# Moving the first stage's arithmetic off GpSimd in a hybrid DeltaNet/HGRN2 step: convolution by pairs of blocks, norm_w folded into x

## The chip, the cores and the metric

One core of a Trainium2 chip runs the whole program. Its engines are the tensor engine (PE, with its weight loads as PEld), the vector engine (DVE), the scalar engine (ACT), GpSimd (POOL) and the sync engine (SP), which here issues every DMA that the program names. Each engine runs its own list of instructions in a fixed order and waits on semaphores. The metric is device time of one execution in microseconds (us).

## The reference, cut to what matters

One layer on a prompt of 4096 tokens (32 tiles of 128) and on a sample of 8 sequences of 16 tokens (one more tile), all in float32. The input x is normed, projected, and split over two groups of heads, whose outputs are joined by one output projection.

```python
h = _rmsnorm(x, norm_w)                   # x * rsqrt(mean(x^2) + eps) * norm_w
proj = h @ w_in
qkv, z_a, b_a, a_a, hq, hf, hi, z_b = jnp.split(proj, offs, axis=-1)
qkv_c = silu(causal depthwise conv of width 4 of qkv)          # 1536 channels
q_a, k_a = l2norm(q) * 64 ** -0.5, l2norm(k)                   # 8 heads of 64
beta, g = sigmoid(b_a), -exp(A_log) * softplus(a_a + dt_bias)
# group A, chunk by chunk, per head: G = cumsum(g), decay[i, j] = exp(G_i - G_j) for i >= j
lower = strict(beta * (k k^T) * decay)
u, w = solve(I + lower, [beta * v, beta * k * exp(G)])
v_new = u - w S;   o = (q * exp(G)) S + ((q k^T) * decay) v_new
S = S * exp(G_last) + (k * exp(G_last - G))^T v_new
# group B (HGRN2): gated linear attention of 4 heads of 128, its own state
y = x + concat(rmsnorm(o_a) * silu(z_a), rmsnorm(o_b) * silu(z_b)) @ w_out;  out = rmsnorm(y)
```

## The kernel before, in words

The program has two phases. **Phase A** norms x, projects q, k, v and the gates of group A, convolves, and runs the delta rule; it also prepares the weights of the second phase. **Phase B** runs HGRN2, the gates and the output projection. Weights and activations are cut into high and low float16 parts, so that a product is three float16 matmuls (`mm3`).

Phase A works on groups: one for the sample tile, then 16 groups of two prompt tiles. For a group g its loop (L285 to L323) issues, in this order of the code: the load and norm of x for g+2 (`xload`), the recurrence of g-1 (`gdn_rec`), decays and score matrices of g (`gdn_pre`), the triangular inverses of g (`gdn_inv`), the transposes of x for g+2 (`xtrans`), the second half of the preparation (`gdn_pre2`), the gates of g+2, the projection and convolution of g+1 (`proj`), and six steps of `wspill`, which reads weights of phase B, scales them and writes their float16 parts to DRAM. A scheduler then puts the instructions of each engine into the order in which the engine runs them; so pieces of neighbouring groups are interleaved, and a small edit can move much.

Names that recur:

- `proj`, L484 to L515: for each of 12 blocks of 128 channels, 24 matmuls into `acc` (L462 to L464). ACT copies the scaled `acc` into `u` (L493) behind three columns of the tile before (`halo`, POOL), makes the tap on the current token from `acc` (`c`, L504) and the oldest tap (`c0`, L507); POOL adds the two (L508); DVE adds the two middle taps (L510); ACT makes the tanh (L512) and DVE the SiLU (L514). `u`, `c`, `c0` and `acc` have two buffers each.
- `gdn_pre`, L517: `E`, [128, 8 heads, 128], comes by a broadcast DMA with G along its free axis; POOL subtracts G of the partition's token (L539) and masks with -1000 (L540); ACT exponentiates (L547). ACT sums squares of k head by head (L554, 8 instructions, each with a read of its accumulator). DVE multiplies the scores by E into `WA` (L573, L574), and SP writes blocks of it to `wdr` in DRAM (L577).
- `gdn_inv`, L605: SP reads `wdr` back as `N` (L623), 64 systems of 32 x 32 on two partitions each. DVE scales N (L632) and eliminates by 31 pairs of instructions, `tm` = column times row (L636), `X` -= `tm` (L638), each of which needs the one before. The scaled `X` (L639) goes by way of DRAM (`xdr`, L646) into `tx` (L654), which DVE transposes into `tT` (L656). `N`, `X`, `tm` and `cs` have one buffer each.
- `gdn_pre2`, L584: squares of q (L594), v times its scale (L600), and on POOL q and k times exp(G) (L602, L603).
- `gdn_rec`, L674: PE, DVE (L713, L723) and ACT in turn apply the inverse; POOL scales the state S (L690), DVE adds to it (L737); squares of the output (L765), a power on POOL (L767), the output `on` (L769).
- `xload`, L362: DVE scales x by its row's norm; norm_w is multiplied into the rows of the weights instead (`wprep` L120, `wspill` L146). In `wspill` POOL also makes the low parts (L185).

## Time and profile before

| | |
|---|---|
| median of 3 runs | 2985.96 us |
| lowest, highest | 2977.22, 2986.02 us |
| profiled execution, first to last instruction | 2983.5 us |
| busy: PE, DVE, ACT, POOL | 2598.1, 1752.2, 1219.2, 991.0 us |
| instructions | 67579 |

The profiled execution's own time is known by its span, 2983.5 us, which is 2.5 us under the median of the runs; what lies around the span is in that difference. A row of the groups' view reads: line, engine, operation, output tile<-input tiles, shapes (partitions x elements, type), count | busy us in all, mean ns of one | idle time of the engine just before them, and what ended it. Phase A fills about the first half of the span, phase B the second.

### The profile page before, as it was taken

To read this page: it belongs to the slowest core of one execution; us is meant where nothing else is said; L and a number is where in the kernel's file an instruction comes from. 1 tells how busy PE (TensorE), PEld (TensorE's weight loads), DVE (VectorE), ACT (ScalarE), POOL (GpSimd) and SP (SyncE) were. 2 spreads that over 40 slices of the span, in tenths; PEclk is the share of its full clock that TensorE was granted. 3 is DMA by queue.
4 is the path that set the end of the run, shared out by engine and by line. 5 is a ranking of instruction groups with operands and counts; after the bars stand their busy time and mean duration, and the time that the engine had idled before them with its cause. 6 is when DMAs were issued, how large, how long until landed. Compare 5 with 4: busy or idle time off the path is not lost.

```text
span 2983.5 us, 67579 instructions
## 1 busy us (share of the span) xinstructions
PE 2598.1 (87%) x27628; PEld 1847.4 (62%) x27628; DVE 1752.2 (59%) x4215; ACT 1219.2 (41%) x3930; POOL 991.0 (33%) x1300
## 2 busy tenths in 40 slices
PE   4768678877877887778899999999999999999997
PEld 4656566665666666666674666666656666665664
DVE  7786778777778788876644434444433344433343
ACT  6656565555555665555332222222222222222222
POOL 5755565465565665655320001110001111000110
PEclk9888999888898989888999999999999999999999
DMA  6334232233343333333233231111110111111010
GB/s 180 100 100 122 68 107 74 73 101 106 98 121 77 96 103 99 97 94 115 77 92 112 73 98 40 43 51 44 51 47 24 46 44 50 44 51 34 32 37 33
DMA packets 298701, 227.78 MB, mean 76 GB/s; under 512 B 186409, under 2 KB 263614, under 8 KB 293782
## 3 DMA queue, kind: packets, MB, share of 16 engines
q1 hardware_dynamic: 298390, 223.45, 25.6%
q8 instruction: 217, 3.56, 0.5%
q14 instruction: 94, 0.77, 0.1%
HBM read 151.78 MB, written 71.62 MB: 75 GB/s over the span
## 4 chain that ended last, share of the span: by engine, by line
PE 49%; DVE 28%; DMA 13%; ACT 2%; issue 2%; POOL 2%; SPq 2%; DVEq 0%; POOLq 0%; ACTq 0%
DMA N<-wdr 7%; DVE X L638 6%; DVE c L510 5%; DVE tm L636 5%; PE py L1016 4%; PE py L1014 4%; PE py L1015 4%; PE hac L462 4%; PE hac L464 4%; PE hac L463 4%; PE sc L954 2%; PE tpzb L1014 2%; PE tpza L1014 2%; PE tpzb L1015 2%; PE tpzb L1016 2%
## 5 line engine op out<-in xcount | busy, mean ns | idle before, releaser
L462 PE MATMUL acc<-xt,w 128*128 128x256 f16 (+1 forms) x1632 | 468.9, 289 | 38.5 <-ACT c L504 36.8
L464 PE MATMUL acc<-xt,w 128*128 128x256 f16 (+1 forms) x1632 | 468.0, 288 | 2.7 <-DVE w L129 2.7
L463 PE MATMUL acc<-xt,w 128*128 128x256 f16 (+1 forms) x1632 | 468.9, 289 | 0.0
L510 DVE SCALAR_TENSOR_TENSOR c<-u,cw,c 128x256 f32<-128x256 f32 (+1 forms) x408 | 237.0, 584 | 31.0 <-POOL c L508 29.8
L1145 DVE SCALAR_TENSOR_TENSOR xr<-py,ysc,xr 128x512 f32<-128x512 f32 x66 | 49.5, 750 | 302.3 <-PE py L1016 302.3
L638 DVE TENSOR_TENSOR X<-X,tm 128x126 f32<-128x126 f32 (+26 forms) x527 | 220.5, 418 | 7.3
L512 ACT ACTIVATE c<-c 128x256 f32<-128x256 f32 (+1 forms) x204 | 83.4, 409 | 322.3 <-DVE c L510 197.6
L463 PEld LDWEIGHTS <-w 128*128 128x128 f16 x1632 | 171.9, 105 | 67.8 <-issue 41.3
L1014 PE MATMUL py<-wo,oh 128*128 128x512 f16 x528 | 201.0, 381 | 4.7 <-ACT oh L1137 3.5
L1016 PE MATMUL py<-wo,ol 128*128 128x512 f16 x528 | 201.1, 381 | 0.2
L1015 PE MATMUL py<-wo,oh 128*128 128x512 f16 x528 | 201.0, 381 | 0.0
L462 PEld LDWEIGHTS <-w 128*128 128x128 f16 x1632 | 172.2, 106 | 37.6 <-issue 9.9
L464 PEld LDWEIGHTS <-w 128*128 128x128 f16 x1632 | 172.0, 105 | 33.5 <-issue 3.3
L636 DVE TENSOR_TENSOR tm<-X,N 128x126 f32<-128x126 f32 (+26 forms) x527 | 187.9, 357 | 7.1
L1048 POOL TENSOR_TENSOR zs<-zs,pw_m 128x1 f32<-128x1 f32 x33 | 20.9, 632 | 469.6 <-DVE zs L1047 469.6
L508 POOL TENSOR_TENSOR c<-c,c 128x256 f32<-128x256 f32 (+1 forms) x204 | 155.9, 766 | 50.9 <-ACT c L507 41.8
L462 PE MATMUL hac<-bxt,whq 128*128 128x256 f16 (+1 forms) x544 | 147.4, 273 | 9.0 <-DVE q L924 9.0
L463 PE MATMUL hac<-bxt,whq 128*128 128x256 f16 (+1 forms) x544 | 147.2, 273 | 0.0
L464 PE MATMUL hac<-bxt,whq 128*128 128x256 f16 (+1 forms) x544 | 147.0, 273 | 0.0
L462 PE MATMUL hac<-bxt,whf 128*128 128x256 f16 (+1 forms) x544 | 145.4, 270 | 0.0
L464 PE MATMUL hac<-bxt,whf 128*128 128x256 f16 (+1 forms) x544 | 145.4, 270 | 0.0
L463 PE MATMUL hac<-bxt,whf 128*128 128x256 f16 (+1 forms) x544 | 145.3, 270 | 0.0
(399 smaller groups left out, 6692.3 us busy)
## 6 DMA issues: line engine op xcount, KB each, us to landing
E<-gdr SPq DMA_DIRECT2D x33, 512.0 KB
out_dram<-xr SPq DMA_DIRECT2D x33, 512.0 KB
x<-in_x_prompt_dram SPq DMA_DIRECT2D x32, 512.0 KB
xd<-xt SPq DMA_DIRECT2D x16, 1024.0 KB
bxt<-xd SPq DMA_DIRECT2D x16, 1024.0 KB
xr<-in_x_prompt_dram SPq DMA_DIRECT2D x32, 512.0 KB
tx<-xdr SPq DMA_DIRECT2D x66, 128.0 KB
oa<-on SPq DMA_DIRECT2D x33, 256.0 KB
```

Of the source, the lines that this page charges most:

```text
L462: nc.tensor.matmul(out, wh[k], xh[k], start=(k == 0), stop=False)
L463: nc.tensor.matmul(out, wh[k], xl[k], start=False, stop=False)
L464: nc.tensor.matmul(out, wl[k], xh[k], start=False, stop=(k == n - 1))
L508: nc.gpsimd.tensor_tensor(c, c, c0, ALU.add)
L510: nc.vector.scalar_tensor_tensor(cv, taps[j], self.cw[:, j, b:b + 1], cv, ALU.mult, ALU.add)
L512: nc.scalar.activation(th, c, AF.Tanh)
L636: nc.vector.tensor_tensor(tv, X[:, 0:R, m:m + 1].to_broadcast([2 * SY, R, c]), N[:, m:m + 1, m + 1:32].to_broadcast([2 * SY, R, c]), ALU.mult)
L638: nc.vector.tensor_tensor(X[:, 0:R, m + 1:32], X[:, 0:R, m + 1:32], tv, ALU.subtract)
L954: nc.tensor.matmul(ps[b:b + 32, k, h], KS[:, k, h, b:b + 32], rhs(k, h, slice(b, b + 32)), start=True, stop=True, tile_position=(0, b))
L1014: nc.tensor.matmul(acc, xh[:, dc], wh[dc], start=(dc == 0), stop=False)
L1015: nc.tensor.matmul(acc, xh[:, dc], wl[dc], start=False, stop=False)
L1016: nc.tensor.matmul(acc, xl[:, dc], wh[dc], start=False, stop=(dc == NDC - 1))
```

## The change

- **norm_w.** A new function `nweights` loads norm_w onto all partitions and scales it by a power of two; `xload` multiplies x by it and by the row's norm in one DVE instruction. The multiplications of the weights' rows on DVE and POOL (L120, L146) go; only the rows of w_out are still scaled, on DVE.
- **wspill.** The high part is a scaled copy on ACT, the low part one DVE instruction in place of one on POOL.
- **Convolution.** Two blocks share one `acc`, `u` and `c`. ACT copies both blocks to `u` in one instruction and makes the oldest tap of each; DVE adds three taps to each block; tanh and SiLU are one instruction each for the two. `c0` and the addition on POOL go.
- **Decay matrix.** Subtraction and mask are one DVE instruction for each head, with a table `cap` of 0 and -1000 that is made once in `masks`.
- **Sums of squares.** One ACT square of 128 x 512 and one DVE reduction (`sums`) take the place of eight ACT instructions with accumulators, for k, q and the output.
- **exp(G)** times q and k is one DVE instruction of 128 x 1024 in place of two on POOL; the **state** S is scaled and added to in eight DVE instructions of 64 x 64 in place of two on POOL and two on DVE.

The core of the diff (comments, renumbered columns and repeated edits are left out):

```diff
+    def nweights(self):
...
+        self.nwb = self.w.tile([P, D], F32, tag="nwb", name="nwb")
+        nc.sync.dma_start(self.nwb, self.i["norm_w"].partition_broadcast(P)[:, 0])
+        m = self.w.tile([P, 3], F32, tag="nwm", name="nwm")
...
+        nc.vector.reciprocal(m[:, 2:3], m[:, 1:2])
+        nc.vector.tensor_scalar(self.nwb, self.nwb, m[:, 2:3], None, ALU.mult)
...
+        self.cap = []
+        for n, m in enumerate((self.mi, self.ms)):
+            self.cap.append(self.w.tile([P, P], F32, tag=f"cap{n}", name=f"cap{n}"))
+            nc.vector.tensor_scalar(self.cap[n], m, 1.0, 1000.0, ALU.subtract, ALU.mult)
...
-        eng.tensor_tensor(st, st, self.nw[:, :, None].to_broadcast([P, NDC, w]), ALU.mult)
...
-            nc.gpsimd.tensor_tensor(st, st, fac[nm][:, :, None].to_broadcast([P, NDC, P]), ALU.mult)
+            if src is wout:
+                nc.vector.tensor_tensor(st, st, wrow[:, :, None].to_broadcast([P, NDC, P]), ALU.mult)
...
-                nc.scalar.copy(hi, st)
+                nc.scalar.activation(hi, st, AF.Copy, scale=fac[nm])
...
-                nc.gpsimd.tensor_tensor(lo, st, hi, ALU.subtract)
+                nc.vector.scalar_tensor_tensor(lo, st, fac[nm], hi, ALU.mult, ALU.subtract)
...
-        nc.vector.tensor_scalar(x, x, ss[:, 1:2], None, ALU.mult)
+        nc.vector.scalar_tensor_tensor(x, x, ss[:, 1:2], self.nwb, ALU.mult, ALU.mult)
...
-        for b in [4, 5, 6, 7, 0, 1, 2, 3, 8, 9, 10, 11]:
-            acc = self.ps_acc.tile([P, 2 * P], F32, tag="acc", name=f"acc{g}_{b}")[:, 0:N]
+        for b in (4, 6, 0, 2, 8, 10):
+
+            acc = self.ps_acc.tile([P, 2, 2 * P], F32, tag="acc", name=f"acc{g}_{b}")[:, :, 0:N]
...
+            for e in range(2):
+                q = slice(e * P, e * P + P)
+                self.mm3(acc[:, e], [wh[:, dc, q] for dc in range(NDC)], [wl[:, dc, q] for dc in range(NDC)], xh, xl)
+            u = self.up.tile([P, 2, 3 + 2 * P], F32, tag="u", name=f"u{g}_{b}")
+            c = self.up.tile([P, 2, 2, P], F32, tag="c", name=f"c{g}_{b}")[:, 0:n]
...
-                nc.scalar.activation(u[:, 3:], acc, AF.Copy, scale=us)
+                nc.scalar.activation(u[:, :, 3:], acc, AF.Copy, scale=us)
...
-            nc.gpsimd.tensor_tensor(c, c, c0, ALU.add)
-            for j in (1, 2):
-                nc.vector.scalar_tensor_tensor(cv, taps[j], self.cw[:, j, b:b + 1], cv, ALU.mult, ALU.add)
...
+            for e in range(2):
+                nc.scalar.activation(cv[e], taps[e][0], AF.Copy, scale=self.cw[:, 0, b + e:b + e + 1])
+            for e in range(2):
+                for j in (1, 2, 3):
+                    nc.vector.scalar_tensor_tensor(cv[e], taps[e][j], self.cw[:, j, b + e:b + e + 1], cv[e],
+                                                   ALU.mult, ALU.add)
...
+            nc.scalar.activation(dst, ck, AF.Tanh)
+            nc.vector.scalar_tensor_tensor(dst, dst, 1.0, ck, ALU.add, ALU.mult)
...
-        nc.gpsimd.tensor_tensor(E, E, d["G"][:, k, :, None].to_broadcast([P, 8, P]), ALU.subtract)
-        nc.gpsimd.affine_select(out=E, in_=E, pattern=[[0, 8], [1, P]], compare_op=ALU.is_ge,
-                                fill=-1000.0, base=0, channel_multiplier=-1)
...
+        for h in range(8):
+            nc.vector.scalar_tensor_tensor(E[:, h], E[:, h], d["G"][:, k, h:h + 1], cap, ALU.subtract, ALU.min)
...
-        for h in range(8):
-            nc.scalar.activation(junk, kt[:, h], AF.Square, accum_out=nrm[:, k, 8 + h:9 + h])
...
+        self.sums(nrm[:, k, 8:16], kt, vs)
...
+    def sums(self, out, x, sq):
+
+        self.nc.scalar.activation(sq, x, AF.Square)
+        self.nc.vector.tensor_reduce(out, sq, AX.X, ALU.add)
...
-        nc.gpsimd.tensor_tensor(kq[:, k, 4:8], kq[:, k, 4:8], eg, ALU.mult)
-        nc.gpsimd.tensor_tensor(kq[:, k, 0:4], kq[:, k, 0:4], eg, ALU.mult)
...
+        nc.vector.tensor_tensor(qk, qk, eg[:, None].to_broadcast([P, 2, 4, P]), ALU.mult)
...
-                nc.gpsimd.tensor_tensor(S[q, :, q], S[q, :, q], el[q, :, DEC_B - 1:].to_broadcast([64, 4, 64]), ALU.mult)
...
-                nc.vector.tensor_tensor(S[q, :, q], S[q, :, q], pss[q], ALU.add)
+                for p in range(4):
+                    nc.vector.scalar_tensor_tensor(S[q, p, q], S[q, p, q], el[q, p, DEC_B - 1:], pss[q, p],
+                                                   ALU.mult, ALU.add)
```

**Where instructions come to stand.** The scheduler makes a new order, and three places of it matter below. Numbers in names tell buffers apart. The first is the elimination on DVE (`tm`, `X`). Before, the start of an inversion looks like this in every group, with instructions of the convolution (`c`) and others between its own:

```order
L632 TENSOR_TENSOR N_6697<-N_6697,cs_6698 128x1024
L600 TENSOR_TENSOR kv_1_6664<-vt_1_6925,sqk_6588 128x512
L636 TENSOR_TENSOR tm_6700<-X_6699,N_6697 128x31
L510 SCALAR_TENSOR_TENSOR c_7_7167<-u_7_7166,cw,c_7_7167 128x256
L638 TENSOR_TENSOR X_6699<-X_6699,tm_6700 128x31
L510 SCALAR_TENSOR_TENSOR c_7_7167<-u_7_7166,cw,c_7_7167 128x256
L596 TENSOR_SCALAR nrm_6587<-nrm_6587 128x8
L636 TENSOR_TENSOR tm_6700<-X_6699,N_6697 128x30
```

In the changed kernel every second group looks like this on DVE: the inversion of one group ends, that of the next begins at once (L644 is the scaling of N, L648 and L650 are the pair), and runs on to its end with almost nothing between:

```order
L648 TENSOR_TENSOR tm_7105<-X_7104,N_7102 128x16
L438 SCALAR_TENSOR_TENSOR h_8408<-h_8408,z_8406 128x16
L650 TENSOR_TENSOR X_7104<-X_7104,tm_7105 128x16
L439 SCALAR_TENSOR_TENSOR h_8408<-h_8408,z_8402 128x16
L651 TENSOR_TENSOR X_7104<-X_7104,cs_7103 128x512
L441 TENSOR_TENSOR h_8408<-h_8408,y_8397 128x16
L443 TENSOR_TENSOR g_8419<-h_8408,negA_84 128x16
L644 TENSOR_TENSOR N_8107<-N_8107,cs_8108 128x1024
L648 TENSOR_TENSOR tm_8110<-X_8109,N_8107 128x31
L650 TENSOR_TENSOR X_8109<-X_8109,tm_8110 128x31
L648 TENSOR_TENSOR tm_8110<-X_8109,N_8107 128x30
```

What moved: the convolution's instructions stand after the inversion there; in the group between, an inversion is spread over some 270 rows.

The second place is on DVE too, between the last scores of a group (`WA`, L574 before, L583 now) and the scaling of N that is made from them. Before:

```order
L574 TENSOR_TENSOR WA_1_7776<-pk_1_1_7784,E_7696 128x2x2x128
L360 TENSOR_SCALAR xss_7988<-xss_7988 128x1
L514 SCALAR_TENSOR_TENSOR kq_8131<-c_6_8240,c_6_8235 128x2x128
L600 TENSOR_TENSOR kv_0_7720<-vt_0_8008,sqk_7694 128x512
L769 TENSOR_TENSOR on_1_6583<-po_1_6499,no_1_6572 128x512
L362 TENSOR_SCALAR x_7986<-x_7986,xss_7988 128x1024
L632 TENSOR_TENSOR N_7803<-N_7803,cs_7804 128x1024
```

Now, in every second group:

```order
L583 TENSOR_TENSOR WA_1_7075<-pk_1_1_7083,E_7001 128x2x2x128
L526 SCALAR_TENSOR_TENSOR c_10_7788<-u_10_7787,cw,c_10_7788 128x2x128
L778 TENSOR_TENSOR on_1_5985<-po_1_5908,no_1_5984 128x512
L526 SCALAR_TENSOR_TENSOR c_10_7788<-u_10_7787,cw,c_10_7788 128x2x128
L389 TENSOR_TENSOR xt_6821<-xtr_0_7271,xt_6821 128x4x128
L526 SCALAR_TENSOR_TENSOR c_10_7788<-u_10_7787,cw,c_10_7788 128x2x128
L389 TENSOR_TENSOR xt_6821<-xtr_1_7278,xt_6821 128x4x128
L201 SCALAR_TENSOR_TENSOR loza_6801<-stza_6797,s2za,hiza_6799 128x1024
L373 TENSOR_SCALAR xss_7287<-xss_7287 128x1
L644 TENSOR_TENSOR N_7102<-N_7102,cs_7103 128x1024
```

What moved: convolution (`c`), a low part of `wspill` (`loza`) and the transposes of x stand between the two now; in the groups of the other kind 100 rows do.

The third place is on SP, where the load of N stands among the other DMAs. Before:

```order
L625 DMA cs_7804<-cdr_7801 128x1x32
L355 DMA x_7986<-in_x_prompt_dram 128x1024
L577 DMA wdr_7695<-WA_1_7776 32x8x32 x4
L623 DMA N_7803<-wdr_7695 128x1x1024
L771 DMA oa<-on_1_6583 128x512
L187 DMA wdza<-hiza_7486 128x8x128
```

Now, in the groups of the other kind:

```order
L203 DMA wdzb<-hizb_7820 128x8x128
L549 DMA E_9011<-gdr_8341 128x1024
L204 DMA wdzb<-lozb_7822 128x8x128
L162 DMA stzb_8807<-in_w_in_dram 128x8x128
L392 DMA xd<-xt_7826 128x4096
L635 DMA N_8107<-wdr_8005 128x1x1024
L658 DMA xdr_189<-X_7104 32x16x32 x4
L637 DMA cs_8108<-cdr_8105 128x1x32
L666 DMA tx_0_7183<-xdr_189 64x8x64 x2
```

What moved: there the load of N is issued behind later loads and just ahead of the write of the X of the group before (`xdr`), and N's one buffer is still read by that group's elimination.

More of the change, by code (lines that the diff above doesn't have):

```diff
@@ L126, in wprep @@
         s2 = small.tile([P, 1], F32, tag="wsc2", name=f"wsd{c0}")
-        self.wscale(tot, us, s2, 1.0 / XS, small, c0)
+        self.wscale(tot, us, s2, small, c0)
         nc.scalar.activation(hi, st, AF.Copy, scale=s2)
@@ L171, in wspill @@
                 us = w.tile([P, 1], F32, tag=f"us{nm}", name=f"us{nm}")
[L172 removed]
+            self.wscale(t1, us, s2, w, nm, src is not wout)
+            fac[nm] = s2
             us5 = w.tile([P, 1], F32, tag=f"u5{nm}", name=f"u5{nm}")
@@ L272, in phase_a @@
             self.G = G
-            self.cw3s = w.tile([P, 12], F32, tag="cw3s", name="cw3s")
-            for b in range(12):
-                nc.vector.tensor_tensor(self.cw3s[:, b:b + 1], self.cw[:, 3, b:b + 1], G[b // 2][2], ALU.mult)
             self.halo = w.tile([P, 12, 3], F32, tag="halo", name="halo")
@@ L592, in gdn_pre2 @@
             nc.tensor.transpose(qt[:, 2 * p:2 * p + 2].rearrange("p a b -> p (a b)"), kq[:, k, p], self.ident)
-        for h in range(8):
-            nc.scalar.activation(junk, qt[:, h], AF.Square, accum_out=nrm[:, k, h:1 + h])
+        self.sums(nrm[:, k, 0:8], qt, self.tp.tile([P, 8, 64], F32, tag="sq", name=f"sq{nm}", bufs=1))
         nc.vector.tensor_scalar(nrm[:, k, 0:8], nrm[:, k, 0:8], 64.0 * EPS, 64.0 * EPS * EPS, ALU.mult, ALU.add)
@@ L687, in gdn_rec @@
                 nc.tensor.matmul(po[:, p * P:(p + 1) * P], kq[:, k, p], S[:, p], start=(p == 0), stop=False)
-            for r in range(2):
-                q = slice(r * 64, r * 64 + 64)
-                nc.gpsimd.tensor_tensor(S[q, :, q], S[q, :, q], el[q, :, DEC_B - 1:].to_broadcast([64, 4, 64]), ALU.mult)
         else:
```

104 lines of the change are left out of this document (46 added, 58 removed).

## The prediction

> **What bounds the kernel now.** I read the span in 40 slices first, then a stretch of ten groups in the windows' view, then what DVE waits for there, and last its groups of instructions.
>
> ```profile
> DVE  7786778777778788876644434444433344433343
> POOL 5755565465565665655320001110001111000110
> PEclk9888999888898989888999999999999999999999
> ```
>
> POOL is busy in the first half alone; there, in phase A, DVE has 7 to 8 tenths, PE's clock is granted at 0.8 to 0.9, and in phase B PE is at 9. So the edit falls into phase A. The first and last start of the scaling of N count its groups:
>
> ```profile
> L632 DVE TENSOR_TENSOR N<-N,cs x17: 1218/1225/1883, 106.3 to 1461.6; 128x1024 f32<-128x1024 f32 x16, 64x1024 f32<-64x1024 f32 x1
> ...
> ```
>
> That is 16 steps in 1355 us. Between two of these starts, 358.5 and 1214.5 us, lie ten groups (columns: us, then busy time and instructions of PE, PEld, DVE, ACT, POOL, clock, DMA share, GB/s):
>
> ```profile
> 358.50:1214.50 856.00, 667.01 (x7536) 544.72 (x7535) 674.74 (x1651) 503.41 (x1833) 496.32 (x653) 0.90 0.34 94
> ```
>
> A group takes 85.6 us; DVE is busy for 67.5 of them and idle for 18.1; PE is busy for 66.7 at a clock of 0.90, ACT for 50, POOL for 50. What DVE waits for in the same stretch:
>
> ```profile
> DVE N L632 <- DMA N<-wdr: 111.0, 11, 13.0
> DVE tT L656 <- DMA tx<-xdr: 26.1, 16, 3.5
> DVE c L510 <- POOL c L508: 19.7, 13, 3.4
> ```
>
> Of the 18.1 idle us 11.1 are the trip of the scores by way of DRAM (`wdr`, N), 2.6 the trip of X, 2.0 the addition on POOL, 2.4 the rest, all small. PE, at 78%, ends few of them. So **a group's time is DVE's stream plus two trips through DRAM**. And DVE's busy time is not all work. Groups of the same stretch, DVE first, then POOL:
>
> ```profile
> L510 DVE SCALAR_TENSOR_TENSOR c<-u,cw,c 128x256 f32<-128x256 f32 x244 | 148.3, 610 | 20.1 <-POOL c L508 19.7
> L638 DVE TENSOR_TENSOR X<-X,tm 128x126 f32<-128x126 f32 (+22 forms) x310 | 138.1, 445 | 3.7
> L636 DVE TENSOR_TENSOR tm<-X,N 128x126 f32<-128x126 f32 (+22 forms) x310 | 106.1, 342 | 3.6
> L514 DVE SCALAR_TENSOR_TENSOR kq<-c,c 128x256 f32<-128x256 f32 x81 | 41.9, 518 | 4.1 <-ACT c L512 3.9
> ...
> L362 DVE TENSOR_SCALAR x<-x,xss 128x1024 f32<-128x1024 f32 x21 | 22.8, 1085 | 4.5 <-POOL xss L361 4.3
> L427 DVE TENSOR_SCALAR y<-y 128x16 f32<-128x16 f32 x10 | 9.0, 904 | 0.0
> ```
>
> ```profile
> L508 POOL TENSOR_TENSOR c<-c,c 128x256 f32<-128x256 f32 x122 | 93.9, 771 | 27.6 <-ACT c L507 21.8 <-DVE tm L636 2.5 <-DVE kv L600 1.8
> L539 POOL TENSOR_TENSOR E<-E,Gc 128x1024 f32<-128x1024 f32 x20 | 39.0, 1949 | 8.5 <-ACT eg L538 6.9 <-DMA E<-gdr 1.5
> L559 POOL TENSOR_TENSOR sqk<-nrm,pw_p 128x8 f32<-128x8 f32 x20 | 34.7, 1733 | 12.9 <-DVE nrm L558 11.9 <-ACT jo L765 0.8
> L767 POOL TENSOR_TENSOR no<-no,pw_m 128x8 f32<-128x8 f32 x20 | 33.4, 1669 | 15.8 <-DVE no L766 15.3
> ...
> L603 POOL TENSOR_TENSOR kq<-kq,eg 128x512 f32<-128x512 f32 x21 | 28.5, 1360 | 4.7 <-PE qt L592 4.7
> ```
>
> The same DVE instructions where POOL rests (timeline, DVE alone: start, us), a pair that POOL's power does not disturb, and an L362 from the chain of waits:
>
> ```profile
> 1410.50 0.29 DVE L636 TENSOR_TENSOR tm<-X,N 128x128 f32<-128x128 f32 x1
> 1410.82 0.29 DVE L638 TENSOR_TENSOR X<-X,tm 128x128 f32<-128x128 f32 x1
> ...
> 1411.70 0.48 DVE L510 SCALAR_TENSOR_TENSOR c<-u,cw,c 128x256 f32<-128x256 f32 x1
> 1412.10 0.28 DVE L636 TENSOR_TENSOR tm<-X,N 128x126 f32<-128x126 f32 x1
> ```
>
> ```profile
> 767.42 1.65 POOL L767 TENSOR_TENSOR no<-no,pw_m 128x8 f32<-128x8 f32 x1
> 768.30 0.41 DVE L514 SCALAR_TENSOR_TENSOR kq<-c,c 128x256 f32<-128x256 f32 x1
> ```
>
> ```profile
> 168.14 0.68 DVE x L362
> ```
>
> A tap (L510) undisturbed lasts 0.48 us and gives way to the next after 0.40; its mean is 0.61. An elimination instruction of 128 elements lasts 0.29; the 62 of an inversion have 92 elements on average, so some 0.25 (36 elements less, at the 1.0 to 1.5 ns an element that lie between 0.29 us for 128 and 0.48 for 256), against means of 0.445 and 0.342. L514 lasts 0.41 against 0.518. That is 244 x 0.13 + 310 x 0.192 + 310 x 0.089 + 121 x 0.11 = 132 us, 13.2 a group. The other rows with operands in SBUF, done in the same way (L362 and L427 are the first and largest of some 25, L427 alone 7 us), give 4 more: 17.2. If each of DVE's instructions is charged its undisturbed start-to-start time, 19.7 of the busy time is left over. I take **18.5 us a group lost to POOL**, so 49.0 of DVE's own.
>
> **The change, part by part.** First what leaves. POOL's additions, E, exp(G), S and weight parts go, POOL's rows with large operands. Left are the powers (L559, L767), halos, the identity X; the power lets L514 pass in 0.41 us, its undisturbed time, so I leave 1.0 of the 18.5. The Trainium skill, page "SBUF — State Buffer", section "Who interferes with whom", says that a DVE instruction with two SBUF inputs and a GpSimd instruction that reads SBUF exclude each other for the whole instruction. By that the powers alone, 3.4 us twice in a group's two tiles, would hold DVE for up to 6.8 us more, an estimate; the row of L514 inside L767 does not bear that out for the power.
>
> What DVE gets, by these rows (the first: four state updates of phase B, the same kind as the new E and S):
>
> ```profile
> 1819.58 1.12 DVE L1098 SCALAR_TENSOR_TENSOR Sb<-Sb,PB,hss 128x128 f32<-128x128 f32 x4 [2.85 <-PE hpo L1076]
> ...
> L1150 DVE SCALAR_TENSOR_TENSOR xr<-xr,ys,fw 128x1024 f32<-128x1024 f32 x27 | 34.5, 1280 | 7.2 <-POOL ys L1149 7.2
> ```
>
> ```profile
> 769.79 0.60 DVE WA L573
> ...
> ```
>
> Four instructions of 128 elements in 1.12 us are 0.26 each; 64 elements less 67 ns: 0.19. L573, 512 elements, moves on after 0.60. Per group of two tiles:
>
> - taps: 36 instead of 24, 12 x 0.40 = +4.8; SiLU 6 of 512 for 12 of 256: 6 x 0.61 - 12 x 0.34 = -0.4
> - E: 16 x 0.26 = +4.2
> - reductions: 6, of 512 elements. The trace has none of that length; by its elements 0.6 as L573, at worst 1.28 as 1024 elements in L1150. I take 0.61: +3.7
> - exp(G): 2 x 1.15 (L632 lasts 1.22, its start-to-start is 0.08 less) = +2.3
> - x: 1.20 (L1150 less 0.08) for 0.68 (L362 undisturbed), twice: +1.0. S: 16 x 0.19 for 4 x 0.40: +1.5
> - low parts and w_out: 28 of 1.20 and 16 of 1.15 over 16 groups, in this stretch 25 and 6: +3.7
> - the inversion that runs alone: two neighbours of 128 elements start 0.32 apart (1410.50, 1410.82), but the next stranger starts 0.20 behind (1412.10 to the row after it, by its duration less 0.08). 0.12 for some 12 more instructions a group on the mean of both kinds: +1.4
>
> Sum +22.2. **DVE's stream: 67.5 - 18.5 + 1.0 + 22.2 = 72.2**, 4.7 more than before.
>
> Then idle time. The trip of the scores, on the chain of waits:
>
> ```profile
> 770.38 0.61 DVE WA L574
> 775.58 13.52 DMA N<-wdr
> 789.12 1.23 DVE N L632
> ```
>
> ```profile
> 840.42 0.70 DVE X L639
> 849.84 0.45 DVE tT L656
> ```
>
> From the end of the scores (770.99) to N 18.1 us pass, 13.5 of them the load. In the order of the changed kernel one kind of group has 4.5 us of DVE's work in between (3 x 0.40 + 3 x 0.60 + 1.2 + 0.1): idle 18.1 - 4.5, less 2 for small waits on the way, 11.6. In the other kind the scores lie 100 rows back, but N's one buffer is read until the last L648, and then the load needs 0.5 for the issue and 13.5, against 2 to 6 us of work: 10. Mean 10.8, for 11.1 before. X to `tT` takes 9 us (841.1 to 849.8) with 4.5 of work in between in one kind, and hides under N's load in the other: 2.3 for 2.6. The waits for POOL go: -2.3. New ones come. E's subtraction now stands in DVE's queue, and waits there for its broadcast, where POOL waited before; behind it stand the scores and the elimination. I price it at +1.5, between nothing and 4. In the inversion that runs alone, the recurrence's DVE steps wait for PE and ACT:
>
> ```profile
> 812.25 1.14 PE L726 MATMUL pz<-r,tx 64*64 64x64 f32 x16 [0.43 <-DVE r L723]
> 813.43 0.58 ACT L727 COPY w<-pz 64x512 f32<-64x512 f32 x1 [0.32 <-PE pz L726]
> ...
> 816.26 0.69 PE L733 MATMUL pss<-w,kv 128*64 128x64 f32 x16
> ```
>
> 1.1 + 0.6 + 0.7 and hand-offs make 2.8 us from L723 to the state, with 2 to 3.5 of work in between; PE often runs other matmuls first (the last row starts 2.2 late): +1.0, between nothing and 3. Idle: 18.1 - 0.3 - 0.3 - 2.3 + 1.5 + 1.0 = 17.7.
>
> **A group: 72.2 + 17.7 = 89.9, +4.3.** Times 16 groups: +69. The start gets shorter by what stood on the chain there:
>
> ```profile
> 16.57 2.29 DVE wst L120
> 32.59 2.20 DVE wst L120
> ```
>
> 4.5 us go; the load and reductions of norm_w give 1.5 back: -3. ACT loses some 17 us a group, which nothing waits for (it is busy for 50 of 85.6), and PE's work stays. Phase B begins after phase A's DVE work and is full of PE's. The sum is made against the profiled 2983.5: 2983.5 + 69 - 3 = 3049.5. The median of the runs lies 2.5 above: **3052 us**.
>
> **Rivals.**
>
> 1. *Faster: POOL's hold is larger than I took.* POOL is busy for 50 us a group and keeps some 13 (below), and a DVE instruction that it delays also delays what PE and ACT hand back to DVE, which stands in the idle time and not in the 18.5. With 22 lost to POOL and 15 idle: 67.5 - 22 + 22.2 + 15 = 82.7, -2.9 a group: 2986 - 46 - 3 = 2937. For it: means in phase A are up to 1.8 times the undisturbed ones (0.445 to 0.25). Against: only what was measured can be given back, and the two trips through DRAM stay.
> 2. *No change:* 18.5 and 22.2 are near; with idle time down to 13.5 a group takes 85.6. 2983.
> 3. *Much slower: the pairs.* Two blocks share one `acc`, `u`, `c`; the taps of a pair stand in DVE's list in chains of six behind one ACT copy, and the inversion that runs alone finds nothing to fill its steps. If each new wait costs its upper price (4 and 3) and the 18.5 is 17.2: 73.5 + 21.2 + 1 for the pairs = 95.7, +10.1: 2986 + 162 - 3 = 3145.
> 4. *The change doesn't do what it says:* what is left on POOL still holds DVE. Powers, halos and identity are some 13 us a group; at half that 6.5 in place of 1.0: 5.5 x 16 = +88 over my sum, 3140. Against it: L514 inside L767. The Trainium skill's rule above would lead to it too.
>
> **How the numbers follow.** Mine 0.48, with a range of its own of 2995 to 3105 (contention 17.2 to 19.7, new waits 0 to 4.5); rival 1 0.32; rival 2 0.08; rival 3 0.09; rival 4 0.03. A measurement of this kernel can tell 0.3%, 9 us, from no change. Slower holds mine, less a little that falls into the middle, and rivals 3 and 4: 0.58; faster 0.33; same 0.09. The range of 8 in 10 reaches from rival 1 to short of rival 3: 2930 to 3115.
>
> **What would show it.** Right: in a stretch of ten groups of phase A, taps near 0.48 us, elimination near 0.25, DVE busy 72 of 90 us, POOL under 15, N's load still the largest wait at 10 to 11 us a group, in both kinds of group. Wrong: a group under 85 us with N's wait gone or halved, or DVE's rows still over 0.5 us; or PE, not DVE's own list, ending DVE's idle time.

## The result

The changed kernel takes 3100.4 us (median of 4 runs, 3098.7 to 3107.1), the kernel before 2984.7 (2977.2 to 2986.0): a ratio of 1.0394, 95% interval 1.0377 to 1.0411. The change makes the kernel 116 us slower; 66 were forecast.

**The profile after.** Three rows of the 40 slices first:

```profile
DVE  7776866768686776967764424443334434333433
POOL 2111111111111121111121010001110100001110
PEclk9986968869678695876889999999999999999999
```

POOL rests, as it should. DVE has the same 7 tenths as before, for longer. PE's clock in phase A, 8 to 9 tenths before, now goes down to 5 and 6 in places. Now the windows' view. The first row is a stretch of ten groups of the changed kernel, from one scaling of N (L644 here) to another, as in the prediction; the second is phase A of the changed kernel, from the first scaling of N to the last, the third the same of the kernel before (columns: us; busy us and instructions of PE, PEld, DVE, ACT, POOL; clock, DMA share, GB/s):

```profile
400.50:1345.20 944.70, 721.68 (x7512) 610.66 (x7512) 709.47 (x2081) 340.79 (x655) 155.74 (x234) 0.79 0.31 85
```

```profile
101.50:1591.10 1489.60, 1130.57 (x11832) 949.43 (x11831) 1102.62 (x3265) 546.83 (x1061) 250.53 (x367) 0.79 0.32 89
```

```profile
106.30:1461.60 1355.30, 1052.63 (x11840) 860.61 (x11841) 1058.55 (x2597) 784.78 (x2837) 769.50 (x1009) 0.89 0.36 98
```

A group takes 94.5 us in the ten (forecast 89.9, before 85.6). DVE is busy for 70.9 of them (forecast 72.2) and idle for 23.5 (forecast 17.7). Over all 16 groups phase A is 134.3 us longer: 44.1 of DVE's busy time and 90.2 of its idle time. **Two thirds of the loss is idle time, of which the forecast had none.** The first scaling of N comes 4.8 us earlier, and what follows the last one is 16.1 us shorter (1521.9 to 1505.8 us): 134.3 - 4.8 - 16.1 = 113.4, the difference of the two spans.

What DVE waits for in the ten groups of the changed kernel:

```profile
DVE N L644 <- DMA cs<-cdr: 105.2, 9, 13.9
DVE r L732 <- PE pcr L731: 18.3, 13, 3.6
DVE E L557 <- ACT eg L554: 15.2, 10, 3.9
DVE tT L668 <- DMA tx<-xdr: 12.4, 11, 4.0
DVE N L644 <- DMA N<-wdr: 9.8, 1, 9.8
DVE kq L531 <- ACT kq L530: 9.3, 4, 4.3
DVE S L747 <- PE pss L742: 8.9, 10, 1.7
DVE r L722 <- PE pks L697: 8.6, 5, 2.6
DVE c L526 <- ACT c L523: 7.2, 9, 1.3
DVE tm L648 <- POOL X L642: 5.9, 4, 1.5
```

The two trips through DRAM are there as before: 11.5 us a group for N (11.1 before) and 1.2 for X (2.6). Nine of the ten waits for N are put down to `cs`, a small load that goes with it; in the chain of waits of the changed kernel it is the load of N itself that lands last (issued at 653.33, it takes 14.01 us, and N starts at 667.4). The wait for POOL's addition is gone. New are PE and ACT: `r` (L732, L722) and S wait for the matmuls of the recurrence, E for ACT's exponential of the same tile (it is overwritten in place), `kq` and `c` for ACT. These six rows are 67.5 us; before, no row of the kind was above 4.3.

The groups of DVE's instructions, and POOL's two powers, in the same stretch:

```profile
L526 DVE SCALAR_TENSOR_TENSOR c<-u,cw,c 128x256 f32<-128x256 f32 x360 | 159.0, 476 | 7.6 <-ACT c L523 7.2
L648 DVE TENSOR_TENSOR tm<-X,N 128x126 f32<-128x126 f32 (+22 forms) x310 | 77.9, 251 | 11.5 <-POOL X L642 5.9
L650 DVE TENSOR_TENSOR X<-X,tm 128x126 f32<-128x126 f32 (+22 forms) x310 | 77.6, 250 | 5.6
L557 DVE SCALAR_TENSOR_TENSOR E<-E,Gc,cap 128x128 f32<-128x128 f32 x160 | 45.4, 344 | 15.2 <-ACT eg L554 15.2
L747 DVE SCALAR_TENSOR_TENSOR S<-S,el,pss 64x64 f32<-64x64 f32 x160 | 35.0, 280 | 9.6 <-PE pss L742 8.9
L375 DVE SCALAR_TENSOR_TENSOR x<-x,xss,nwb 128x1024 f32<-128x1024 f32 x20 | 25.5, 1276 | 0.2 <-POOL xss L374 0.2
L615 DVE TENSOR_TENSOR kq<-kq,eg 128x1024 f32<-128x1024 f32 x20 | 24.3, 1216 | 0.0
L596 DVE TENSOR_REDUCE nrm<-sq 128x8 f32<-128x512 f32 x20 | 13.5, 675 | 0.0
```

```profile
L568 POOL TENSOR_TENSOR sqk<-nrm,pw_p 128x8 f32<-128x8 f32 x20 | 35.9, 1796 | 155.0 <-DVE nrm L567 147.1 <-DVE e L427 7.8
L777 POOL TENSOR_TENSOR no<-no,pw_m 128x8 f32<-128x8 f32 x20 | 33.8, 1689 | 25.9 <-DVE xss L373 19.1 <-DVE no L776 5.2 <-DVE ctr L570 1.4
```

A tap lasts 476 ns on the mean (0.48 undisturbed), the elimination 251 and 250 (forecast 0.25). Next to nothing holds DVE any more.

**Where the new idle time is.** In the changed kernel the inversions are of two kinds, as its order showed. The windows' view over five of each, from the scaling of N to the last X, one window and the sum; first the short ones, then the long ones, then five of the kernel before:

```profile
778.40:807.00 28.60, 19.64 (x270) 16.39 (x270) 20.74 (x75) 4.79 (x12) 2.49 (x3) 0.62 0.09 20
sum 138.20, PE 97.00 PEld 81.62 DVE 104.26 ACT 21.66 POOL 15.23; mean PE 19.40 PEld 16.32 DVE 20.85 ACT 4.33 POOL 3.05
```

```profile
667.40:763.60 96.20, 84.50 (x826) 72.67 (x827) 89.29 (x267) 47.32 (x86) 16.21 (x27) 0.89 0.43 125
sum 474.00, PE 419.33 PEld 358.08 DVE 437.92 ACT 226.60 POOL 83.02; mean PE 83.87 PEld 71.62 DVE 87.58 ACT 45.32 POOL 16.60
```

```profile
702.10:749.90 47.80, 37.91 (x375) 31.31 (x376) 46.83 (x120) 25.39 (x76) 28.79 (x38) 0.88 0.35 107
sum 240.10, PE 197.11 PEld 162.13 DVE 231.99 ACT 141.94 POOL 140.87; mean PE 39.42 PEld 32.43 DVE 46.40 ACT 28.39 POOL 28.17
```

Before, DVE was busy for 97% of an inversion; now for 92% in the long ones and 75% in the short ones, where PE's clock is 0.62 to 0.87. In phase A the idle time inside inversions rose from 23 us to 109, about half in each kind (summed over DVE's rows). That is 86 of the 90 us: the new idle time lies inside the inversions, and the time between them has no more of it than before.

### The profile page after: what moved, and what is told of

Same layout as the page of the kernel before. It is cut to its first block, busy times and chain, and to the rows that moved or that the text cites. A ratio compares the mean times of both kernels' runs of the same rounds, so it can differ in the third digit from the quotient of the medians.

```text
span 3096.9 us, 65439 instructions
## 1 busy us (share of the span) xinstructions
PE 2667.2 (86%) x27628; PEld 1934.8 (62%) x27628; DVE 1795.6 (58%) x4933; ACT 968.1 (31%) x2043; POOL 416.6 (13%) x608
## 4 chain that ended last, share of the span: by engine, by line
PE 57%; DVE 17%; DMA 14%; ACT 3%; SPq 3%; issue 2%; POOL 1%; POOLq 0%; ACTq 0%; DVEq 0%
DVE c L526 4%; PE py L1025 4%; PE py L1023 4%; PE py L1024 4%; PE hac L475 3%; PE hac L477 3%; PE hac L476 3%; DMA E<-gdr 3%; PE sc L963 2%; PE acc L476 2%; PE acc L477 2%; PE acc L475 2%; PE tpza L1023 2%; DMA cs<-cdr 2%; PE tpza L1024 2%
## 5 line engine op out<-in xcount | busy, mean ns | idle before, releaser
L475 PE MATMUL acc<-xt,w 128*128 128x256 f16 (+1 forms) x1632 | 451.2, 280 | 20.4 <-ACT xt L388 14.0
L476 PE MATMUL acc<-xt,w 128*128 128x256 f16 (+1 forms) x1632 | 452.4, 280 | 0.0
L477 PE MATMUL acc<-xt,w 128*128 128x256 f16 (+1 forms) x1632 | 451.9, 280 | 0.1
L526 DVE SCALAR_TENSOR_TENSOR c<-u,cw,c 128x256 f32<-128x256 f32 (+1 forms) x612 | 265.0, 467 | 12.7 <-ACT c L523 12.0
L475 PEld LDWEIGHTS <-w 128*128 128x128 f16 x1632 | 165.9, 102 | 42.4 <-issue 18.4
L476 PEld LDWEIGHTS <-w 128*128 128x128 f16 x1632 | 166.6, 102 | 31.2 <-issue 9.0
L477 PEld LDWEIGHTS <-w 128*128 128x128 f16 x1632 | 166.6, 102 | 24.3 <-issue 2.2
L648 DVE TENSOR_TENSOR tm<-X,N 128x126 f32<-128x126 f32 (+26 forms) x527 | 132.7, 252 | 18.4 <-POOL X L642 8.7
L650 DVE TENSOR_TENSOR X<-X,tm 128x126 f32<-128x126 f32 (+26 forms) x527 | 132.2, 251 | 9.9
L1025 PEld LDWEIGHTS <-bxt 128*128 128x128 f16 x792 | 77.8, 98 | 92.3 <-issue 1.9
L580 PE MATMUL pk<-kq 64*128 64x256 f32 x528 | 102.1, 508 | 38.2 <-DVE WA L583 30.6
L1024 PEld LDWEIGHTS <-bxt 128*128 128x128 f16 x792 | 77.8, 98 | 89.4 <-issue 7.5
```

Of the source, the lines that this page charges most:

```text
L475: nc.tensor.matmul(out, wh[k], xh[k], start=(k == 0), stop=False)
L476: nc.tensor.matmul(out, wh[k], xl[k], start=False, stop=False)
L477: nc.tensor.matmul(out, wl[k], xh[k], start=False, stop=(k == n - 1))
L526: nc.vector.scalar_tensor_tensor(cv[e], taps[e][j], self.cw[:, j, b + e:b + e + 1], cv[e], ALU.mult, ALU.add)
L580: nc.tensor.matmul(pk[:, r, pp], kq[q, k, 4 + p], kq[q, k, p:8:4], start=True, stop=True)
L648: nc.vector.tensor_tensor(tv, X[:, 0:R, m:m + 1].to_broadcast([2 * SY, R, c]), N[:, m:m + 1, m + 1:32].to_broadcast([2 * SY, R, c]), ALU.mult)
```

## The experiments

All kernels below are rebuilt by the scheduler, so that each has an order of its own; a difference between two is the price of the edit with the order that comes with it. The table has them all. Phase A is the time from the first to the last scaling of N. In conv_first, two_N_late and before_late_N the first scaling of N itself comes 24 to 45 us later than before, so there the medians decide. "Held" is the part of DVE's busy time beyond the undisturbed start-to-start time of the same instruction, an estimate that moves by 10 to 30 us with the times that are taken as undisturbed. The last three columns are DVE's waits for the two trips, its waits for PE and ACT, and PE's granted clock in phase A. All times are in us.

| run | median | ratio to before, 95% | phase A | DVE busy | held | idle | N, tT | PE + ACT | clock |
|---|---|---|---|---|---|---|---|---|---|
| before | 2984.7 | | 1355 | 1059 | 292 | 297 | 219 | 32 | 0.89 |
| after | 3100.4 | 1.0394 (1.0377 to 1.0411) | 1490 | 1103 | 19 | 387 | 209 | 132 | 0.79 |
| before_light_POOL | 2827.0 | 0.9485 (0.9464 to 0.9505) | 1218 | 801 | 50 | 416 | 186 | 124 | 0.91 |
| conv_first | 3203.2 | 1.0740 (1.0719 to 1.0761) | 1557 | 1113 | 28 | 444 | 251 | 126 | 0.76 |
| two_N | 3104.2 | 1.0410 (1.0392 to 1.0428) | 1489 | 1106 | 20 | 384 | 181 | 114 | 0.78 |
| two_N_late | 3101.4 | 1.0394 (1.0379 to 1.0410) | 1456 | 1079 | 20 | 377 | 38 | 205 | 0.78 |
| before_late_N | 3042.2 | 1.0184 (1.0166 to 1.0202) | 1385 | 1044 | 249 | 341 | 51 | 165 | 0.86 |
| E_on_POOL | 3065.4 | 1.0282 (1.0261 to 1.0302) | 1447 | 1095 | 71 | 351 | 159 | 138 | 0.81 |
| single_blocks | 3062.8 | 1.0262 (1.0246 to 1.0277) | 1447 | 1106 | 20 | 341 | 185 | 109 | 0.84 |
| sums_on_ACT | 3040.5 | 1.0185 (1.0157 to 1.0213) | 1428 | 1051 | 25 | 378 | 171 | 152 | 0.81 |
| E_sums_blocks_undone | 2975.3 | 0.9976 (0.9961 to 0.9992) | 1347 | 1047 | 85 | 300 | 157 | 108 | 0.87 |
| conv_and_weights_only | 2957.2 | 0.9907 (0.9893 to 0.9922) | 1336 | 1027 | 121 | 309 | 189 | 76 | 0.87 |
| weights_and_taps | 2949.8 | 0.9884 (0.9857 to 0.9910) | 1324 | 1036 | 135 | 288 | 172 | 70 | 0.89 |
| weights_only | 2937.1 | 0.9848 (0.9820 to 0.9876) | 1319 | 1023 | 196 | 296 | 181 | 57 | 0.88 |

### What POOL's work is worth: before_light_POOL

```diff
-            nc.gpsimd.tensor_tensor(c, c, c0, ALU.add)
+            nc.gpsimd.tensor_tensor(c[:, 0:1], c[:, 0:1], c0[:, 0:1], ALU.add)
...
-        nc.gpsimd.tensor_tensor(kq[:, k, 4:8], kq[:, k, 4:8], eg, ALU.mult)
+        nc.gpsimd.tensor_tensor(kq[:, k, 4:5, 0:8], kq[:, k, 4:5, 0:8], eg[:, 0:1, 0:8], ALU.mult)
```

> The kernel before with POOL's arithmetic that the change takes away cut to 8 columns or fewer (the convolution's addition, E's subtraction and mask, exp(G), the scaling of S, the weights' rows; the low parts of phase B's weights are zeros); this part of the computation is left out, DVE, PE and ACT keep their instructions. Theory of the forecast: DVE gets back 17.5 us of busy time a group and the 2.0 us of waits for L508, 85.6 becomes 66 to 69 us a group where PE (66.7 us busy) begins to end it: 2983 - 16 x 17 to 19.5 = 2670 to 2715 us. Rival, the hold only fills time in which DVE would wait for its two trips anyway: less than half comes back, 2850 us and more.

This run leaves out nearly all of POOL's large operands, so its outputs are not the program's. 2827 us, 158 less, between the two theories and nearer to the rival. Ten groups of it, in the windows' view, in the groups of instructions and in DVE's waits:

```profile
332.40:1095.40 763.00, 638.29 (x7501) 531.15 (x7501) 509.71 (x1648) 496.74 (x1816) 230.74 (x648) 0.92 0.39 107
```

```profile
L510 DVE SCALAR_TENSOR_TENSOR c<-u,cw,c 128x256 f32<-128x256 f32 x243 | 116.4, 479 | 34.0 <-POOL c L508 32.3
L636 DVE TENSOR_TENSOR tm<-X,N 128x126 f32<-128x126 f32 (+22 forms) x310 | 78.2, 252 | 3.8
L638 DVE TENSOR_TENSOR X<-X,tm 128x126 f32<-128x126 f32 (+22 forms) x310 | 78.1, 252 | 4.1
```

```profile
DVE c L510 <- POOL c L508: 32.3, 30, 3.2
DVE kq L514 <- ACT c L512: 20.5, 18, 3.3
```

The busy time fell as forecast: from 67.5 to 51.0 us a group, and the elimination takes the 252 ns that it takes where POOL rests. But a group only fell from 85.6 to 76.3. Over phase A 257 us of busy time went and 120 of idle time came, 92 of them as waits for PE and ACT and 37 as waits for POOL's shortened instructions, with no work added anywhere. So **about half of what DVE was freed of came back as waits**. My reading is that this was covered time: held by POOL, DVE came late to results of PE and ACT that were then ready; freed, it comes early and waits.

### Order or trips: conv_first, two_N, two_N_late, before_late_N

```diff
                 if 0 <= g + 1 < ng:
-                    self.proj(g + 1, st[g + 1])
+                    with tc.high_priority(2000):
+                        self.proj(g + 1, st[g + 1])
```

> The changed kernel with the same instructions; only the scheduler's priority of the convolution (proj) is raised by 2000, so that all groups get one order: about 102 DVE rows between the scaling of N and the last X in every group, where the changed kernel has 67 to 83 in one kind of group and 170 to 230 in the other. Theory order: the 5.9 us a group of idle time that DVE has beyond the forecast (23.6 for 17.7) and the 47 us that the first three groups took longer come from the two kinds of groups; with one kind a group takes 86 to 90 us and the program 2990 to 3040 us. Theory work: DVE's own stream and its waits for PE are what they are in any order: 3080 to 3110 us.

3203 us: neither, and the theory of the order falls as I put it. All groups are of one kind, and yet a group is slower. DVE's waits in ten groups:

```profile
DVE N L645 <- DMA cs<-cdr: 93.2, 8, 13.8
DVE tT L669 <- DMA tx<-xdr: 55.6, 14, 10.3
```

Over phase A the wait for the trip of X rose from 26 us in the changed kernel to 79, while that for N stayed (183 and 172): with the convolution done early, DVE has little left to put behind the trip of X, which takes 5.6 us a group here. One kind of group is not what the kernel before had; it had convolution spread through the inversion. That the two kinds cost the time is therefore not shown, and not refuted either.

```diff
-        N = self.ex.tile([P, 32, 32], F32, tag="N", name=f"N{g}")[0:2 * SY]
+        N = self.ex.tile([P, 32, 32], F32, tag="N", name=f"N{g}", bufs=2)[0:2 * SY]
```

> The changed kernel with two buffers for N and for cs, nothing else. Theory buffer: in every second group the load of N waits for the elimination before it to give N free; with a second buffer that group's wait (about 11 us of it) goes, 5 to 6 us a group in the mean, so 3100 - 16 x 5.5 = about 3010 us. Theory trip: the wait moves on, to the trip of X and to the matmuls that the tight elimination leaves behind, and less than a third of it comes back: 3070 to 3100 us.

3104 us, no gain: the theory of the trip. With two buffers the load is early, the scheduler then puts the scaling of N earlier too, and in the next step `X` with its one buffer is waited for:

```profile
DVE N L644 <- DMA cs<-cdr: 92.1, 8, 16.1
DVE tm L648 <- POOL X L642: 13.0, 3, 6.3
```

The next two hold the scaling of N back in DVE's list, in both kernels:

```diff
+            if prev and b == 11:
+                self.tc.add_manual_dep(prev["Ns"].ins, last.ins.name,
+                                       mybir.DependencyInfo(mybir.DependencyClass.NoSync, mybir.DependencyReason.DATA),
+                                       reason="N behind the convolution")
...
-        nc.vector.tensor_tensor(N, N, cs[:, :, None].to_broadcast([2 * SY, 32, 32]), ALU.mult)
+        d["Ns"] = nc.vector.tensor_tensor(N, N, cs[:, :, None].to_broadcast([2 * SY, 32, 32]), ALU.mult)
```

> The kernel before with the same instructions; the scaling of N of group g is put behind the last SiLU of the convolution of g+1 in DVE's list (an order edge, no wait of its own), so that by the lengths of DVE's rows 14 to 23 us of work stand between the scores and N in place of 2 to 4. Theory order: the trip of the scores takes about 18 us and DVE has other work for that time, but the list puts N in front of it; N's wait falls from 10.3 us a group to under 4 and a group from 85.6 to about 79: 2983 - 16 x 6 = about 2890 us (2860 to 2920). Rival trip: another wait takes its place (X to tT, PE with 66.7 busy us, the convolution waiting for ACT and POOL): 2960 to 2990 us or more.

> The changed kernel with two buffers for N and cs, and the scaling of N behind the last SiLU of the next group's convolution, as in the run before_late_N: 10 to 30 us of DVE's rows between the scores and N in every group. With two buffers alone N still waited 10.0 us a group, since its scaling stood close behind the scores again. Theory order: N's wait falls to under 4 us a group, 3104 - 16 x 6 = about 3010 us. Rival PE and ACT: the waits for PE and ACT (6 us a group now against 2 before) grow by what N gives back, 3080 us and more.

N's wait went, from 174 us in phase A to 14 and from 156 to 11, and the time did not: 3042 us for the kernel before, 57 more, and 3101 for the changed one, 3 less than with two buffers alone. Ten groups take 897.5 us for 856.0 in the kernel before, and 957.2 for 943.3 in the changed one. What DVE waits for instead, ten groups of the first and of the second:

```profile
DVE c L510 <- POOL c L508: 49.8, 18, 13.0
DVE ba L405 <- ACT ba L404: 23.0, 2, 12.0
DVE vv L514 <- ACT c L512: 20.3, 13, 12.5
```

```profile
DVE xss L373 <- ACT xt L370: 38.6, 5, 14.5
DVE tm L652 <- POOL X L646: 23.8, 4, 7.2
```

So the 11 us of N's wait are not idle time that this order picks up; whether another would is open. By these rows, DVE's other work at that point is fed by ACT and POOL and is not ready any sooner; that the others catch up while DVE waits for N is how I read them.

### The parts of the change

Three parts undone singly, each as its lines in the kernel before:

```diff
-        for h in range(8):
-            nc.vector.scalar_tensor_tensor(E[:, h], E[:, h], d["G"][:, k, h:h + 1], cap, ALU.subtract, ALU.min)
+        nc.gpsimd.tensor_tensor(E, E, d["G"][:, k, :, None].to_broadcast([P, 8, P]), ALU.subtract)
+        nc.gpsimd.affine_select(out=E, in_=E, pattern=[[0, 8], [1, P]], compare_op=ALU.is_ge,
+                                fill=-1000.0, base=0, channel_multiplier=-1)
```

> The changed kernel with the subtraction and mask of E on POOL again, as before (two POOL instructions of 128 x 1024 a tile in place of eight on DVE). DVE loses 16 instructions of 0.27 us and their wait for the broadcast (4.3 + 1.5 us a group) and gets POOL's hold back (2 x 3.6 us of POOL time a group, at about half: 3 to 3.5). Theory sum: 2.3 to 2.8 us a group less, 3055 to 3065 us. Theory queue: E in DVE's queue is what upset the order and the waits behind it; without it 6 us a group and more are back, under 3010 us. A third outcome, no gain (3090 and more), would say that POOL's hold is worth as much as the work.

3065 us, 35 less: the theory of the sum, at its edge.

```diff
-        for b in (4, 6, 0, 2, 8, 10):
+        for b in (4, 5, 6, 7, 0, 1, 2, 3, 8, 9, 10, 11):
...
-            u = self.up.tile([P, 2, 3 + 2 * P], F32, tag="u", name=f"u{g}_{b}")
+            u = self.up.tile([P, 1, 3 + 2 * P], F32, tag="u", name=f"u{g}_{b}")
```

> The changed kernel with the convolution by single blocks again (12 acc, u and c of one block, one copy, one tanh and one SiLU for each), the three taps on DVE kept. DVE has 12 SiLU instructions of 256 elements for 6 of 512: +0.4 us a group. Rival of the pairs: sharing acc, u and c by two blocks is what costs the time beyond the sum; single blocks give 2 to 3 us a group back, 3050 to 3070 us. Theory of the sum: pairs neither cost nor save much, 3095 to 3115 us.

3063 us, 38 less: **the pairs cost 2.3 us a group**, as their rival said. Not by work (DVE is busy for 1106 us and 1103): the idle time falls from 387 to 341, 23 of it waits for PE and ACT, 24 the two trips, and PE's clock rises from 0.79 to 0.84. What is held stays (20 and 19).

```diff
-        self.nc.scalar.activation(sq, x, AF.Square)
-        self.nc.vector.tensor_reduce(out, sq, AX.X, ALU.add)
+        for h in range(8):
+            self.nc.scalar.activation(sq[:, h], x[:, h], AF.Square, accum_out=out[:, h:h + 1])
```

> The changed kernel with the sums of squares of k, q and the output on ACT's accumulators again (eight ACT instructions a sum in place of one ACT and one DVE instruction); DVE loses 6 reductions of 0.60 a group. By the term: 3100 - 16 x 3.6 = about 3042 us. If half of what DVE is freed of turns into waits: 3070 us. If less work on DVE also ends waits elsewhere (the five parts undone so far gave more together than apart): under 3010 us.

3041 us, 60 less, where the term is 58. The reductions cost their length; this one is work alone (52 us of DVE's busy time, 9 of idle).

Then several parts at a time, down to one:

```diff
-        nc.vector.tensor_tensor(qk, qk, eg[:, None].to_broadcast([P, 2, 4, P]), ALU.mult)
+        for a in (1, 0):
+            nc.gpsimd.tensor_tensor(qk[:, a], qk[:, a], eg, ALU.mult)
...
-                for p in range(4):
-                    nc.vector.scalar_tensor_tensor(S[q, p, q], S[q, p, q], el[q, p, DEC_B - 1:], pss[q, p],
-                                                   ALU.mult, ALU.add)
+                nc.vector.tensor_tensor(S[q, :, q], S[q, :, q], pss[q], ALU.add)
```

> The changed kernel with E, exp(G), the scaling of S on POOL again and the sums of squares on ACT's accumulators again; what is left of the change is the convolution, norm_w and the preparation of weights. By the terms of the forecast DVE loses 4.2 + 1.5 (E), 2.3 (exp(G)), 1.4 (S) and 3.6 (sums) = 13.0 us a group and gets POOL's hold back: 2 x (3.6 + 2.6 + 0.6) us of POOL's time a group at the measured 16.5 us of hold for 38 of POOL, 0.43, are 5.9; so 7.1 us a group less, 3100 - 114 = about 2987 us. If the order matters beyond that (all groups are of about one kind here, 35 to 45 us of rows from N to X), the waits inside the inversions go back too, another 3 us a group: about 2940 us. If POOL's hold eats it: 3020 us and more.

2957 us, below the sum and above the more hopeful figure: 143 under the changed kernel, and **faster than the kernel before** (0.9907, 0.9893 to 0.9922).

> conv_and_weights_only with the convolution by single blocks: of the change there remain norm_w in x, the preparation of phase B's weights, and the third tap on DVE in the place of POOL's addition. Additive theory: the pairs cost 37 us here as they did in the changed kernel (3100 to 3063), 2957 - 37 = 2920 us (2910 to 2935). Rival: the pairs only cost where DVE's list is long enough that their longer steps delay what is behind; here they cost nothing, 2950 to 2965 us.

2950 us. Here the pairs cost 7 us and not 38: the rival. That their price depends on how full DVE's list is fits these two prices, and nothing else here shows it.

> The changed kernel with E on POOL, sums on ACT and single blocks; exp(G) and the scaling of S stay on DVE. Against weights_and_taps this leaves 2.3 + 1.4 us a group more on DVE and takes 2 x (2.6 + 0.6) us of POOL's time a group away, 2.8 of hold at 0.43. By full terms +0.9 a group, 15 us above weights_and_taps; with half of the hold +2.3, 37 us above; 60 us and more if the waits behind DVE's longer list add up as in the changed kernel.

2975 us, 26 above weights_and_taps, between the full terms (15) and half of the hold (37). So exp(G) and S on DVE lose too. Against the kernel before, 207 us of hold are gone here (292 to 85), DVE is busy for about as long (1047 and 1059), and its idle time is the same (300 and 297).

```diff
-                for j in (1, 2, 3):
+            nc.gpsimd.tensor_tensor(c, c, c0, ALU.add)
...
+                for j in (1, 2):
```

> weights_and_taps with the convolution of the kernel before (POOL's addition, two taps on DVE): of the change there remain norm_w in x and the preparation of phase B's weights. By full terms DVE loses 12 x 0.40 = 4.8 us a group and gets back the hold of 9.4 us of POOL time at 0.43, 4.0, and 1.6 us of waits for POOL: +0.8 a group, 13 us above weights_and_taps. If half of a hold is time in which DVE would wait anyway (as in before_light_POOL, where 270 us of hold gave 156 back): 4.0 counts 2.1, so -1.1 a group, 18 us below it. So this run tells whether taking the addition off POOL paid at all.

2937 us, 13 below: nearer to the theory of half of the hold (18 below) than to full terms (13 above). Taking the addition off POOL did not pay. Phase A of this kernel in the windows' view:

```profile
103.40:1422.30 1318.90, 1060.93 (x11861) 865.98 (x11860) 1022.90 (x2624) 742.94 (x2827) 645.85 (x926) 0.88 0.36 100
```

DVE is busy for 36 us less than before and idle for as long; the rest is 9.4 us behind the last N and 3 ahead of the first. This is the fastest version that computes the whole program, **48 us or 1.5% under the kernel before** (0.9848, 0.9820 to 0.9876).

The steps, in medians: 2984.7 before; norm_w and the weights -48; the third tap +13; exp(G) and S +26; then E, sums and pairs together +125, where their single undoings come to 35 + 60 + 38 = 133. So the parts nearly add up, and **all of the gain is in the weights, and every part that moved work of the delta rule or the convolution to DVE lost**.

## Why the prediction was right, and where its size was off

- **Side: right; mechanism: a third of the loss.** The kernel is slower, and DVE's stream does lose POOL's hold and gain as much work and more: 44 of phase A's 134 us. The other 90 are idle time, which the forecast had falling by 6.
- **That 3100 lies within 2995 to 3105 is partly luck.** The upper end allows phase A some 122 us more (3105 - 2986 + 3), and it grew by 134. The 16 us that came back behind the last N, which had no term in the sum, brought the time inside again.
- **The hold.** I took 18.5 of a group's busy time as lost to POOL and left 1.0. By the same accounting 19.3 us are left in phase A, 1.2 a group. The two powers are busy for 7.0 us a group here (L568, L777), and the rival by which they hold DVE falls. The Trainium skill, page "SBUF — State Buffer", section "Who interferes with whom", has a DVE instruction with two SBUF inputs contend with a GpSimd instruction that reads SBUF, for ports that are locked and not shared out; for the 128 x 8 power the trace of the changed kernel does not agree, since all of DVE's hold there, 1.2 us a group, is smaller than the powers' 7.0.
- **The added work.** 22.2 were forecast. DVE's own time rose from 47.8 us a group to 69.7 in the ten groups, 21.9. The reductions, without a row of their kind before, were taken at 0.61 and take 0.60 from start to start; the run sums_on_ACT has them at their term.
- **Idle time: the step that failed.** "18.1 - 0.3 - 0.3 - 2.3 + 1.5 + 1.0 = 17.7" came to 23.5. N was near (11.5 for 10.8), X better (1.2 for 2.3), E at its price (1.5). The waits of the recurrence, taken at +1.0 with 3 as the upper price, are 3.6 (L732, L722, S). And two terms were left out: ACT's tap and tanh (`c`, `kq`: 1.6), and POOL's identity X, which a short inversion waits for (0.6). Where they come from is shown in part. The pairs, put at nothing in the sum, are 46 of the 90 us of new idle time (387 to 341 in single_blocks, with the hold unchanged); with E back on POOL 36 go, with the sums back on ACT 9. That the hold went is not the reason by itself: before_light_POOL, where nothing took its place, has 120 us of new idle time, but E_sums_blocks_undone, where as much work did, has 3. Each of these runs has an order of its own; how much each new wait owes to the order and how much to PE's lower clock stays open.
- **The pairs: a rival's mechanism, in part.** I priced them at nothing in the sum and put "1 for the pairs" into rival 3. They cost 2.3 us a group in the full change. The recurrence's waits came too, at 3.6 for its upper price of 3. The rest of that rival did not: E's wait was 1.5 and not 4, and the work was not more. Its sum is off by one: with the two upper prices, 17.7 becomes 22.2 and not 21.2, so it stands for 96.7 us a group and 3161 us.
- **Times 16.** Ten groups cost 8.9 us more each, the first three 47 us together, the last three 1 less. Over all 16 the busy time rose by 44 us, not 75, and the idle time by 90, not -6. 16 us behind the last N, not forecast, came back. What shortens that part is open; it was 3 to 16 us shorter in every other run as well.
- **The faster rival** wanted a hold of 22 and idle time of 15. The hold was 19.7 at most, and idle time rose.

What stays open: whether the two kinds of group cost anything by themselves (conv_first changed more than that), and how much of the longer waits for PE comes from its lower clock.

## What to carry to other kernels

Taking away the instructions of an engine that hold up another gives back the busy time that the rows show, and part of it can turn into waits. Here that was half where nothing took their place, and one run with their work cut to nothing shows it before anything is moved. When a change has many parts, price each: one part that gains 48 us was hidden under others that lost 163. A large wait at the head of an engine's list need not be time to win: holding the waiting instruction back moved 160 us of wait to other rows and made the kernel slower.

## What the runs showed of the hardware

PE's granted clock fell with the change, though PE's work did not. With the same matmuls it was 0.89 in phase A before and 0.79 after, and PE's busy time there rose from 1053 to 1131 us. It was 0.62 to 0.87 in the five short inversions, where PE is busy for 70% of the time, and 0.83 to 0.89 in the long ones (88%) and in those of the kernel before (82%). In a short one the 16 matmuls of one step of the recurrence take, in PE's timeline:

```profile
796.03 1.97 PE L727 MATMUL py<-r,tx 64*64 64x64 f32 x16 [0.78 <-DVE r L722]
```

1.97 us, where a step of the same 16 shapes took 1.14 in the row of the kernel before that the prediction shows. The clock over the first is 0.50 (796.0 to 798.1), around the second 1.00 (811.0 to 814.0). These are single steps. On the mean of ten groups the matmuls of the two steps are 18 to 20% longer, first before, then after:

```profile
L726 PE MATMUL pz<-r,tx 64*64 64x64 f32 x320 | 26.0, 239 | 15.3 <-DVE r L723 15.2
L718 PE MATMUL py<-r,tx 64*64 64x64 f32 x320 | 24.6, 230 | 12.8 <-DVE r L713 12.7
```

```profile
L735 PE MATMUL pz<-r,tx 64*64 64x64 f32 x320 | 34.4, 286 | 13.5 <-DVE r L732 13.5
L727 PE MATMUL py<-r,tx 64*64 64x64 f32 x320 | 31.9, 272 | 44.4 <-DVE r L722 44.2
```

So the chain that DVE waits for gets longer with the lower clock. The windows' view of a stretch in one short inversion:

```profile
799.00:808.40 9.40, 7.79 (x86) 7.22 (x85) 6.82 (x26) 1.78 (x3) 0.00 (x0) 0.50 0.00 0
```

The clock is 0.50 there. The Trainium skill, page "TensorE: Matmul & The Clock Gate", section "Part 1: The HAM clock gate (the "warmup" mystery)", has the throttled clock, half of full speed, as the default, which sustained activity lifts; the rows of the short and the long inversions agree. By that rule the lower clock is an effect of PE's gaps. The prediction took PE's work as it stood and did not ask what the new order does to PE. Among the runs, those with DVE idle for about 300 us in phase A have a clock of 0.87 to 0.89, and those with 341 and more 0.76 to 0.86; before_light_POOL (416 us, 0.91) does not fit this, and no run here set the clock apart from the rest.
